# All transfers of a dilated convolution moved into one fixed order on one DMA queue

## Chip, cores, metric

One core of one Trainium2 chip. The metric is the device time of one execution in microseconds (us). Ratios in this text are computed as the mean time of one kernel's fast runs over the mean time of the fast runs of the kernel before in the same rounds on the same chip, so they are not quite the ratio of the medians that stand beside them. Some executions of a kernel run slower than the rest: one that is over 1.5% above the fastest of its kernel is called slow here (the slow state). Slow runs are left out of the ratios, but not out of the medians. The interval beside a ratio is its 95% interval.

## The reference

A 3x3 convolution with dilation 2 and padding 2, in float32: 16 images of 64 channels of 64x64, to 128 output channels.

```python
x_pad = np.pad(x, ((0, 0), (0, 0), (pad, pad), (pad, pad)), mode='constant')   # pad = 2
for b, co, ci, kh, kw in ...:                     # loops, cut
    output[b, co] += weight[co, ci, kh, kw] * x_pad[b, ci, kh*2:kh*2+h, kw*2:kw*2+w]
```

16.8 MB of images and 0.3 MB of weights come in, 33.55 MB go out.

## The kernel before

Two images make a pair (64 + 64 channels fill the 128 partitions); a pair is computed in four groups of 16 rows, 32 groups in all. Each group's sums go through three PSUM tiles, of which DVE adds two to a copy of the third (`p_sb`, made by ACT) into the output tile. Inputs arrive as float32 (`x32`, 3 buffers, 2 MB each) and are cast by ACT to float16, a quarter of a pair at a time (`cast(c)`, c counts quarters). Output tiles have 3 buffers of 4 MB.

```python
def load(pb, cuts=(0, H), queue=nc.sync):
    x32_tiles[pb] = fpool.tile([P, HW], f32, tag="x32", name="x32")
    for lo, hi in zip(cuts[:-1], cuts[1:]):
        queue.dma_start(out=x32_tiles[pb][:, lo * W : hi * W], in_=x_pair[pb, :, lo * W : hi * W])
# ... cut: at the start SyncE's queue gets the weights, pair 0 in two pieces, pair 1, pair 2

def casts(G):                                   # called in each group G
    for n in range(2 if G else 3):
        c = ahead[0]
        if c >= ngroups or c > G + (7 if c < 2 * NG else 3):
            return
        cast(c)
        ahead[0] += 1
        if c % NG == NG - 1 and c // NG + XF < npairs:      # pair fully cast: its x32 buffer is free
            k = c // NG + XF
            load(k, (0, H) if k < 6 else (0, H // 2, H), queue=nc.scalar)
# ... cut: products
    if not G:
        casts(0)
    p_sb = spool.tile([P, 2 * NH], f32, tag="psb", name="p_sb")
    nc.scalar.copy(out=p_sb, in_=psP)
    if G:
        casts(G)
# ... cut: row sums and output adds on DVE
    if pb == npairs - 1:
        ...                                     # last pair: stores in half images, one piece of it cut
                                                # into 124 + 4 partitions (FOUR, of ROWS4 = 8 rows)
    elif g == NG - 1:
        store(pb, 0)                            # SyncE's queue, 2 MB each
        store(pb, 1)
```

So there are two queues: stores (and the first loads) on SyncE's, the loads of pairs 3 to 7 on ScalarE's.

## Time and profile before

| | before |
|---|---|
| time, median of 3 | 127.12 us (127.10 to 127.21) |
| profiled execution | 128.3 us, span 126.5 us |
| data moved | 50.78 MB |
| PE busy | 105.1 us, 83% |

The page of the kernel before; the rows cut the span in 40 slices of 3.16 us, digits are tenths of busy time:

```profile
PE   6894999999999999999999999999999999300000
DMA  4999999999999999999999999999999999999960
GB/s 137 375 447 435 430 425 435 425 300 430 414 420 451 430 420 425 409 446 430 417 438 414 422 420 435 427 435 420 440 420 425 440 420 440 414 412 416 426 266 23
...
q1 hardware_dynamic: 3448, 40.14, 75.4%
q10 hardware_dynamic: 1008, 10.49, 20.4%
...
PE 75%; DMA 6%; ACT 2%; issue 1%; DVE 1%; DVEq 1%; SPq 1%; ACTq 0%
```

Two engines look full. The chain of waits is three quarters PE. But look where PE stops: at slice 34 of 40, while the DMA row stays at 9 to slice 38. The chain, in order of time, ends at the last DVE add and does not follow the stores behind it:

```profile
106.14 1.28 PE psA L174 x12
...
107.52 1.23 DVE osb L237
108.74 1.13 DVEq L287
```

The stores (SyncE's queue, duration in ns, then the first and last start in us):

```profile
L188 SPq DMA_DIRECT2D out_dram<-osb x20: 332/450/1606, 23.3 to 110.3; - x20
```

The last is issued at 110.3 us, and 12 us of transfers are still queued. So the DMA engines look like what sets the time, and PE could be late by some us without harm (before_casts5 below tests that). The windows of the kernel before show one hole in a DMA stream that otherwise runs at 428 GB/s with loads alone (4 to 20 us):

```profile
core 0: us, PE busy (x) PEld busy (x) DVE busy (x) ACT busy (x) POOL busy (x), PEclk, DMA share, GB/s
22.00:24.00 2.00, 2.00 (x24) 1.18 (x22) 1.83 (x4) 1.01 (x1) 0.00 (x0) 1.00 1.04 442
24.00:26.00 2.00, 2.00 (x22) 1.06 (x20) 2.00 (x2) 0.38 (x1) 0.00 (x0) 1.00 1.03 385
26.00:28.00 2.00, 2.00 (x23) 1.08 (x20) 1.58 (x3) 1.68 (x2) 0.00 (x0) 1.00 0.98 270
...
123.00:124.00 1.00, 0.00 (x0) 0.00 (x0) 0.00 (x0) 0.00 (x0) 0.00 (x0) 0.50 0.16 66
124.00:125.00 1.00, 0.00 (x0) 0.00 (x0) 0.00 (x0) 0.00 (x0) 0.00 (x0) 0.50 0.06 25
```

At 26:28 the DMA share is 0.98, yet only 270 GB/s move: the engines are busy with packets that take longer. This text calls it the slow stretch. At 124:125 the share is 0.06, one engine of sixteen: a straggler.

### The profile page before, as it was taken

Reading aid. Unit: us, or ns where it says so; the run is one execution under the profiler, and the core shown is the slowest. Engines: PE = TensorE matmul, PEld = TensorE weight load, DVE = VectorE, ACT = ScalarE, POOL = GpSimd, SP = SyncE. Lnnn points to the kernel's source line nnn. Section 1 sums busy time; section 2 is a strip of 40 time slices with the busy share of each in tenths; the row PEclk is TensorE's granted clock in tenths of the full one; section 3 lists DMA queues with packets and bytes.
Section 4 is the critical chain, followed back from the end, with each engine's and each line's share of the span. In section 5 each row is a group of like instructions: output and inputs, shape, how many; then the busy total and the mean of one; then the engine's idle time right before and its main releaser. Section 6 shows DMA issues by size and latency. Waiting matters only on the chain.

```text
span 126.5 us, 2335 instructions
## 1 busy us (share of the span) xinstructions
PE 105.1 (83%) x1000; PEld 56.2 (44%) x1000; DVE 90.7 (72%) x103; ACT 65.0 (51%) x68; POOL 2.3 (2%) x8
## 2 busy tenths in 40 slices
PE   6894999999999999999999999999999999300000
PEld 2251555555555555555555555555556555100000
DVE  0560998988898889898969898888888887700000
ACT  4287893366656665766486666666666533000000
POOL 2400000000000000000000000000000000000000
PEclk9999999999999999999999999999999999965555
DMA  4999999999999999999999999999999999999960
GB/s 137 375 447 435 430 425 435 425 300 430 414 420 451 430 420 425 409 446 430 417 438 414 422 420 435 427 435 420 440 420 425 440 420 440 414 412 416 426 266 23
DMA packets 4466, 50.78 MB, mean 401 GB/s; under 512 B 488, under 2 KB 488, under 8 KB 1000
## 3 DMA queue, kind: packets, MB, share of 16 engines
q1 hardware_dynamic: 3448, 40.14, 75.4%
q10 hardware_dynamic: 1008, 10.49, 20.4%
q8 instruction: 8, 0.13, 0.4%
q14 instruction: 2, 0.02, 0.0%
HBM read 17.07 MB, written 33.55 MB: 400 GB/s over the span
## 4 chain that ended last, share of the span: by engine, by line
PE 75%; DMA 6%; ACT 2%; issue 1%; DVE 1%; DVEq 1%; SPq 1%; ACTq 0%
PE psA L174 30%; PE psB L174 29%; PE psP L174 16%; DMA x<-in_x_dram 6%; DVE osb L237 1%; DVEq L287 1%; ACT p_sb L230 1%; ACT x L73 1%; SPq L64 0%; ACTq L64 0%; SPq L88 0%; DVEq L237 0%
## 5 line engine op out<-in xcount | busy, mean ns | idle before, releaser
L174 PEld LDWEIGHTS <-w_sb 64*128 64x128 f16 x960 | 54.2, 94 | 46.9 <-issue 2.1
L230 ACT COPY p_sb<-psP 128x1024 f32<-128x1024 f32 x32 | 32.4, 1012 | 37.5 <-PE psP L174 18.1
L237 DVE TENSOR_TENSOR osb<-psA,p_sb 128x1024 f32<-128x1024 f32 x32 | 39.2, 1224 | 14.2 <-PE psA L174 8.4
L174 PE MATMUL psA<-x,w_sb 64*128 64x496 f16 (+3 forms) x384 | 45.1, 365 | 0.0
L174 PE MATMUL psB<-x,w_sb 64*128 64x496 f16 (+3 forms) x384 | 45.1, 365 | 0.0
L237 DVE TENSOR_TENSOR osb<-psB,p_sb 128x1024 f32<-128x1024 f32 x32 | 39.1, 1221 | 0.0
L73 ACT CAST x<-x 128x1024 f16<-128x1024 f32 (+2 forms) x31 | 32.1, 1044 | 0.4 <-DMA x<-in_x_dram 0.4
L174 PE MATMUL psP<-xs,w_sb 64*128 64x496 f16 (+1 forms) x192 | 26.0, 371 | 1.8 <-ACT p_sb L230 1.8
L85 DVE TENSOR_TENSOR xs<-x 128x512 f16<-128x512 f16 x32 | 13.3, 416 | 0.7 <-ACT x L73 0.7
L101 PE MATMUL dm<-zero 128*128 128x512 f16 x10 | 4.6, 580 | 1.2 <-DVE zero L93 1.2
L111 DVE CAST wd<-w 128x192 f16<-128x192 f32 x1 | 0.5, 507 | 2.6 <-DMA w<-in_weight_dram 2.6
L101 PEld LDWEIGHTS <-zero 128*128 128x128 f16 x10 | 1.1, 123 | 2.6 <-issue 1.3
L124 PEld LDWEIGHTS <-wd 128*64 128x64 f16 x30 | 1.0, 118 | 2.3 <-DVE wd L111 1.2
L124 PE MATMUL wt<-ident,wd 128*64 128x128 f16 x30 | 1.6, 241 | 0.3 <-DVE wd L111 0.3
L113 ACT ACT_TABLE_LOAD x1 | 1.3, 1283 | 0.7 <-PEq L273 0.7
L136 ACT CAST w_sb<-wt 128x384 f16<-128x384 f32 x1 | 0.5, 480 | 1.8 <-PE wt L124 1.8
L113 ACT CAST wd<-w 128x192 f16<-128x192 f32 x1 | 0.5, 542 | 1.7 <-DMA w<-in_weight_dram 1.7
L138 DVE CAST w_sb<-wt 128x384 f16<-128x384 f32 x1 | 0.6, 558 | 0.9 <-PE wt L124 0.9
L93 DVE MEMSET zero<- 128x256 uint32 x1 | 0.3, 272 | 0.9 <-PEq L273 0.9
L112 POOL TENSOR_TENSOR wd<-w 128x192 f16<-128x192 f32 x1 | 0.8, 801 | 2.5 <-DMA w<-in_weight_dram 2.5
L115 POOL CAST wd<-w 128x192 f16<-128x192 f32 x1 | 0.8, 815 | 0.0
L114 DVE TENSOR_TENSOR wd<-w 128x192 f16<-128x192 f32 x1 | 0.8, 799 | 0.0
(11 smaller groups left out, 3.6 us busy)
## 6 DMA issues: line engine op xcount, KB each, us to landing
out_dram<-osb SPq DMA_DIRECT2D x14, 2048.0 KB, 17.4
x<-in_x_dram ACTq DMA_DIRECT2D x3, 2048.0 KB, 14.6
x<-in_x_dram SPq DMA_DIRECT2D x2, 2048.0 KB, 11.7
x<-in_x_dram ACTq DMA_DIRECT2D x4, 1024.0 KB, 19.9
out_dram<-osb SPq DMA_DIRECT2D x3, 1024.0 KB, 14.1
x<-in_x_dram SPq DMA_DIRECT2D x1, 1088.0 KB, 5.5
x<-in_x_dram SPq DMA_DIRECT2D x1, 960.0 KB, 7.3
out_dram<-osb SPq DMA_DIRECT2D x1, 768.0 KB, 15.6
```

Of the source, the lines that this page charges most:

```text
L73: nc.scalar.copy(out=x16_tiles[pb][:, lo * W : hi * W], in_=x32_tiles[pb][:, lo * W : hi * W])
L85: nc.vector.tensor_tensor(out=s, in0=v[:, :, 0], in1=v[:, :, 1], op=add)
L101: nc.tensor.matmul(out=dm[:, 0:512], lhsT=zero[:, 0:P], rhs=zero)
L112: nc.gpsimd.tensor_tensor(out=wdv[:, 3], in0=wv[:, 0], in1=wv[:, 1], op=sub)
L113: nc.scalar.copy(out=wdv[:, 2], in_=wv[:, 0])
L114: nc.vector.tensor_tensor(out=wdv[:, 1], in0=wv[:, 2], in1=wv[:, 1], op=sub)
L115: nc.gpsimd.tensor_copy(out=wdv[:, 4], in_=wv[:, 2])
L124: nc.tensor.matmul(out=wts[k % 3][r * CI : (r + 1) * CI, c0 + j * CO : c0 + (j + 1) * CO], lhsT=wd[:, t * CI : (t + 1) * CI], rhs=ident,)
L174: nc.tensor.matmul(out=po, lhsT=w_sb[pp, t * CO : (t + 1) * CO], rhs=rhs, start=first and j == 1, stop=last and j == 2,)
L230: nc.scalar.copy(out=p_sb, in_=psP)
L237: nc.vector.tensor_tensor(out=o[:, :, b0 : b0 + NBLK, e], in0=ps.rearrange("p (m b q) -> p m b q", m=2, q=2 * W), in1=pv, op=add,)
L287: with _tile.TileContext(nc) as tc:
```

## The change

The intent: one queue, so that each transfer runs at full rate in a chosen order, none slowed by a later one: four pairs in, the first pair out in halves with the fifth pair's load behind it, then a load and two stores in turn. Casts from pair 2 on may run two groups earlier, so that buffers come free in time.

```diff
-    def load(pb, cuts=(0, H), queue=nc.sync):
+    def load(pb, cuts=(0, H)):
...
-            queue.dma_start(
+            nc.sync.dma_start(
...
-            if c >= ngroups or c > G + (7 if c < 2 * NG else 3):
+            if c >= ngroups or c > G + (7 if c < 2 * NG else 5):
                 return
             cast(c)
             ahead[0] += 1
-            if c % NG == NG - 1 and c // NG + XF < npairs:
-                k = c // NG + XF
-                load(k, (0, H) if k < 6 else (0, H // 2, H), queue=nc.scalar)
...
-        if pb == npairs - 1:
+        if G == 0:
+            load(XF)
+        if g == NG - 1 and 0 < pb < npairs - XF - 1:
+            load(pb + XF + 1)
+        if pb in (0, npairs - 1):
             if g % 2 == 1:
                 store(pb, 0, (g - 1) * GR, (g + 1) * GR)
-                if g == 1:
+                if pb and g == 1:
...
+            if G == NG - 1:
+                load(XF + 1)
         elif g == NG - 1:
```

## The prediction

> **What bounds the kernel now.** The DMA engines. In the 40-slice page DMA reads 9 from slice 2 to slice 38, at 410 to 450 GB/s. The kernel moves 50.34 MB of data; at the rate of its steady stretches (426 GB/s in 64:93 mixed, 428 GB/s in 96:119 with stores alone, 428 GB/s early with loads alone) that is 118 us of the 126.5 us span. The rest: 1.6 us before the first packet, about 1 us at the start (302 to 348 GB/s in 2:5 while the weights come in small packets), a dip to about 306 GB/s in 25:28 (windows) in which the engines are busy but x packets take 0.7 to 1.36 us instead of 0.61 (worth about 0.9 us), and about 4 us after 122 us, where a straggling engine drains and the last receipt comes in. The Trainium skill ("DMA: Bandwidth & Descriptors", Specifications) puts the fabric ceiling at 435 GB/s; the trace agrees with 426 to 428.
>
> The chain of waits is 75% PE, but it ends there at 107 to 109 us; the last store is issued at 110.3 us and what is left is the DMA backlog, 5 MB or 12 us.
>
> **What the change does.** Same bytes, same packets in size (loads split into 8 KB a partition become whole, the first pair's stores become 8 KB: as many). The seven loads leave ACT's queue; each cost ACT 0.33 us of issue (two of them 1.1 and 1.5 us). Only one is on the PE chain: 0.38 us at 10.9 us, ahead of the first p_sb copy; compute starts about 0.4 us earlier, hidden by the DMA backlog. Casts of pair 2 start two groups earlier.
>
> The skill (same page, "Issuing engines are not separate DMA queues") says both queues run on the same 16 engines and interleave; one queue should not change the rate. In this trace mixed and single-queue stretches differ by under 1%.
>
> **Does the fixed order open a gap?** Costed from bytes moved by the time each store comes ready: at 17.3 us (first half of pair 0 done) about 2.2 MB of loads are still queued; at 23 us 2.0 MB; at 35.5 us (pair 1) over 3 MB, against 1.3 MB before; at 97.5 us (pair 6) 2.2 MB, 5 us. The loads waiting for casts 11, 15 and 19 come free at about 31, 43 and 56 us, before their turn. Output buffers come free 3 us or more before reuse. I expect no idle gap on the DMA engines, no new PE wait, and the PE end within 1 us of 108.5.
>
> **The gain** can then only be the dip at 25:28, at most 0.9 us. It sits just after the first stores were issued (23.3 us) beside a load on the other queue. If it is the price of the first writes it returns; if the meeting of two queues, it goes. Half each: minus 0.45 us. 127.12 - 0.45 gives about 126.7 us.
>
> **Signs.** Right: DMA 9 in slices 2 to 38; GB/s near 428 in every steady stretch; q10 gone; last store issue near 110 us. Wrong: a slice of DMA below 8 in the middle (starved queue), PE waits on x loads, or the output add waiting for a store.
>
> **What would make it wrong.** A transfer held behind one that isn't ready; switching between loads and stores costing rate; the straggling engine at the end moving by over 1 us.
>
> Predicted 126.7 us, 8 in 10 between 125.7 and 127.8; faster by over 2% 0.05, within 2% 0.91, slower 0.04.

(A recount of the trace gives 427 GB/s in 64:93 and 422 in 96:119, where the prediction has 426 and 428; mixed and single-queue stretches then differ by up to 1.5%, not by under 1%. By our estimate that adds 0.3 us to the 118 us of its sum: 23 us at 422 in place of 428.)

## The result, and the profile after

| | before | after |
|---|---|---|
| time, median (same rounds) | 127.16 us (127.10 to 127.43, 4 runs) | 126.75 us (126.67 to 127.05, 4 runs) |
| ratio of the fast runs | | 0.9968, 95% interval 0.9946 to 0.9989 |
| profiled execution | 128.3 us | 126.76 us |
| last store issued | 110.3 us | 109.6 us |

The same within 2%; the gain is 0.4 us. (The profiled run of before was 1.2 us slower than its median, so spans of the two traces are not to be subtracted.) The page after:

```profile
PE   6996999999999999999999999999999999400000
DMA  4999999899999999999999999999999999999991
GB/s 145 373 427 456 435 420 399 299 425 422 446 438 430 425 420 440 422 430 420 435 425 433 430 430 430 420 425 425 446 430 425 430 420 425 425 433 411 424 387 76
...
q1 hardware_dynamic: 4456, 50.63, 96.6%
...
PE 76%; DMA 6%; ACT 2%; DVE 1%; DVEq 1%; SPq 1%; issue 0%
```

q10 (ScalarE's queue) is gone; the DMA row is full as before. The chain ends 0.7 us earlier (DVE's last step in it at 106.77 in place of 107.52), and so does the last store's issue (109.6 for 110.3; in the second pair of traces, before_again and after_again, 110.1 for 111.0):

```profile
106.77 1.23 DVE osb L234
108.00 1.13 DVEq L290
```

```profile
L185 SPq DMA_DIRECT2D out_dram<-osb x22: 332/432/712, 16.6 to 109.6; - x22
```

Where compute gained is seen at its start. Before, ScalarE issued a load between its last cast and the first `p_sb` copy; after, the copy follows the cast at once (both timelines are cut at 10.5 us):

```profile
9.96 0.93 ACT L73 CAST x<-x 128x896 f16<-128x896 f32 x1
10.92 0.38 ACTq L64 DMA_DIRECT2D x<-in_x_dram  x1
11.34 1.01 ACT L230 COPY p_sb<-psP 128x1024 f32<-128x1024 f32 x1 [0.45 <-ACT x L73]
```

```profile
9.76 0.93 ACT L73 CAST x<-x 128x896 f16<-128x896 f32 x1
10.60 1.00 ACT L227 COPY p_sb<-psP 128x1024 f32<-128x1024 f32 x1
```

The windows after:

```profile
20.00:22.00 2.00, 2.00 (x24) 1.14 (x21) 1.82 (x2) 1.19 (x2) 0.00 (x0) 1.00 1.25 393
22.00:24.00 2.00, 2.00 (x24) 1.12 (x20) 1.83 (x3) 1.86 (x2) 0.00 (x0) 1.00 0.66 217
24.00:26.00 2.00, 2.00 (x22) 1.08 (x20) 1.80 (x3) 1.08 (x2) 0.00 (x0) 1.00 1.01 426
...
123.00:124.00 1.00, 0.00 (x0) 0.00 (x0) 0.00 (x0) 0.00 (x0) 0.00 (x0) 0.50 0.10 41
124.00:125.00 1.00, 0.00 (x0) 0.00 (x0) 0.00 (x0) 0.00 (x0) 0.00 (x0) 0.50 0.00 0
```

The slow stretch is there again, at 21 to 24 us, now with a single queue. (A packet counts in the window where it starts, so a share over 1 ahead of one under 1 is long packets, not idleness.) The straggler ends sooner in this trace; by how much differs from run to run, as the table below shows. One new wait showed, in the timeline of DVE:

```profile
85.24 1.23 DVE L234 TENSOR_TENSOR osb<-psA,p_sb 128x1024 f32<-128x1024 f32 x1 [0.52 <-DMA out_dram<-osb]
```

An output buffer came free 0.5 us late. It will have cost nothing here, as the stores queued at the end are much longer than that.

Three numbers are used below, all worked out from the packet records of each trace. *Slow time*: for the 20 to 30 us stretch, the sum over packets of what each took over its usual time (611 ns for 16 KB, 309 ns for 8 KB, the medians), divided by the 16 engines. *Last engine*: the end of the last packet. *Mean engine*: the ends of the last 16 semaphore packets (4 bytes each, one for each engine), averaged. Where a second number stands, it is a further stretch outside 20 to 30 us. The profiled runs:

```
kernel                   run us   slow time us   mean engine   last engine   run - last
before                   128.30   1.00           122.67        125.37        2.93
before_again             127.86   1.04           122.85        124.79        3.07
before_casts5            127.54   1.08           122.59        124.47        3.07
after                    126.76   1.02           122.36        123.82        2.94
after_again              127.06   1.10           122.62        123.99        3.07
old_order_one_queue      127.03   1.01           122.51        124.00        3.03
old_order_one_queue_2    127.65   1.01           122.70        124.71        2.94
after_early_store        127.87   0.94           122.58        124.74        3.13
after_early_store_sp     128.78   0.98           122.75        125.73        3.05   (slow state)
after_half_four          127.08   1.00           122.50        124.01        3.07
after_casts3             127.62   0.79 + 0.90    123.21        124.58        3.04   (second stretch at 42 us)
after_store_first        127.89   1.90           123.54        124.96        2.93   (two stretches)
new_order_two_queues     130.48   1.04 + 1.24    125.48        127.56        2.92   (slow state; more at 38 to 47 us)
after_early_bulk         130.80   1.87 + 0.48    126.46        127.74        3.06   (two, and one at 9 to 14 us; 2.4 us more of data)
```

In every trace the run's time is the last engine's end plus 2.9 to 3.1 us. So the time is the DMA engines' work, with whatever the slowest of the sixteen adds. Leaving out the two slow runs and the last kernel with its extra data, that last part (last engine less mean engine) goes from 1.4 to 2.7 us.

### The profile page after: what moved, and what is told of

It reads as the page before. It is cut to its first block, busy times and chain, and to the rows that moved or that the text cites. A ratio compares the mean times of both kernels' runs of the same rounds, so it can differ in the third digit from the quotient of the medians.

```text
span 125.0 us, 2339 instructions
## 1 busy us (share of the span) xinstructions
PE 105.1 (84%) x1000; PEld 56.0 (45%) x1000; DVE 90.8 (73%) x103; ACT 64.9 (52%) x68; POOL 2.2 (2%) x8
## 4 chain that ended last, share of the span: by engine, by line
PE 76%; DMA 6%; ACT 2%; DVE 1%; DVEq 1%; SPq 1%; issue 0%
PE psA L171 31%; PE psB L171 30%; PE psP L171 16%; DMA x<-in_x_dram 6%; ACT x L73 2%; DVE osb L234 1%; DVEq L290 1%; ACT p_sb L227 1%; SPq L64 0%; SPq L88 0%; DVEq L234 0%
## 6 DMA issues: line engine op xcount, KB each, us to landing
out_dram<-osb SPq DMA_DIRECT2D x12, 2048.0 KB, 19.3
```

## The experiments

Twelve further runs were made, of nine edited kernels (one of them twice) and of the two kernels unedited; all gave correct results. One more kernel, the two-queue version of the changed one with the old cast limit, was not run, and nothing of it is on record. The author gives as the reason a deadlock, which the program's order bears out: the load of pair 5 stands in ScalarE's program at the end of group 7, where the old limit has let casts up to number 10 through, and it would wait for cast 11 behind it. So with two queues this order needs the earlier casts.

### Controls: after_again and before_again

No edit. For the changed kernel:

> Control, the changed kernel once more, for a tighter ratio and a second trace. Expected: ratio to the kernel before 0.996 to 0.998, the slow stretch of loads (rate under 300 GB/s for about 2 us) again at 21 to 24 us just ahead of the first store packets, worth 1.0 us per DMA engine. If the 0.3% gain was chance, the ratio is 1.000 within 0.001.

Median 126.99 us against 127.22, ratio 0.9969, interval 0.9924 to 1.0014; slow time 1.10 us at 21 to 24 us. For the kernel before:

> Control: the kernel before, twice. Ratio 1.000 within 0.002; what it differs by is the noise of such a comparison. Its second trace: slow stretch at 25 to 28 us, 1.0 us; the last DMA engine ends about 3.0 us before the run's time, near 124.2 us (the first trace, of a run 1.2 us above the median, had 125.4).

Median 127.82 against 127.36, ratio 1.0014, interval 0.9978 to 1.0050. The runs spread more here than in the first comparison (126.95 to 128.02 for the kernel before, against 127.10 to 127.43). The last engine ended at 124.8, not 124.2, in a run 0.5 us above the median. The gain of 0.3% came out in two comparisons with the same point value, but its second interval holds 1: it is at the edge of what such runs resolve.

### Queue or order: old_order_one_queue and its repeat

```diff
-                load(k, (0, H) if k < 6 else (0, H // 2, H), queue=nc.scalar)
+                load(k, (0, H) if k < 6 else (0, H // 2, H), queue=nc.sync)
```

> The kernel before with its loads issued from SyncE at the same places of the program: one queue, old order and old cast schedule. Theory Q (the gain is the single queue: loads and stores no longer share each DMA engine packet by packet): ratio 0.997. Theory O (the gain is the order of the transfers, or the earlier casts): ratio 1.000. Both: slow stretch stays, 1.0 us.

127.35 us, ratio 0.9990, interval 0.9936 to 1.0045; runs from 126.59 to 128.62, too noisy. The slow time was 1.01 us, at 26 to 29 us. The ten traces at hand by then suggested a theory: the last engine ended 1.4 to 1.5 us behind the mean wherever only one queue was used, 1.9 to 2.7 where two were. The repeat was to test it:

> Repeat of the old order on one queue, whose first timing was too noisy. Theory Q (the gain is the single queue, through a more even finish of the 16 DMA engines): ratio 0.995 to 0.998, the last engine ends 1.3 to 1.6 us after the mean of the engines (with two queues it was 1.9 to 2.7). Theory O (the gain is the order): ratio 1.000, 1.9 us or more.

127.12 us against 127.33, ratio 0.9988, interval 0.9955 to 1.0021. The last engine ended 2.0 us behind the mean. The ratio lies between the two theories and its interval holds both, and the number that theory Q named came out on the wrong side. So did a later trace, after_early_bulk below, with two queues and 1.3 us. Over all twelve fast traces, six of the seven with one queue have 1.4 to 1.5 us and one has 2.0; four of the five with two have 1.9 to 2.7 and one has 1.3. The present run and three of those four were 0.3 to 1.2 us above their kernel's median, so the lag may belong to a slower run and not to the queues. That theory is not kept.

### New order, two queues: new_order_two_queues

```diff
-            load(XF)
+            load(XF, queue=nc.scalar)
...           # the same for load(pb + XF + 1) and load(XF + 1)
```

> The changed kernel with its fourth to eighth loads on ScalarE's queue at the same places of the program. Theory Q: ratio 1.000 (gain gone). Theory O: 0.997 (gain kept). Both: slow stretch stays, 1.0 us.

128.42 us (slow runs up to 130.6 included), ratio 1.0047, interval 0.9986 to 1.0107: it holds theory Q's 1.000 and not theory O's 0.997. But something else happened in this kernel too, so it tests neither. ScalarE's timeline and a window of the profiled run show it. (That run was slow. The wait is not told from this run alone: the next experiment shows it in a fast one.)

```profile
19.19 1.01 ACT L227 COPY p_sb<-psP 128x1024 f32<-128x1024 f32 x1 [0.42 <-ACT x L73]
26.14 1.15 ACT L73 CAST x<-x 128x1152 f16<-128x1152 f32 x1 [5.94 <-DMA x<-in_x_dram]
```

```profile
24.00:26.00 2.00, 0.50 (x6) 0.11 (x2) 0.00 (x0) 0.00 (x0) 0.00 (x0) 1.00 0.95 401
26.00:28.00 2.00, 0.00 (x0) 0.00 (x0) 0.00 (x0) 1.86 (x2) 0.00 (x0) 0.82 0.99 418
```

The first cast of pair 2 is wanted at 20 us, and ScalarE waits 5.9 us for its input; with it the `p_sb` copies wait, and PE stands idle through 26:28. The fourth load, on its own queue, takes its turns on the DMA engines beside the third: by the packet records the third pair's last packet ended at 25.2 us here, at 18.4 us in the changed kernel. PE ended at 114.9 us, against 107.8 in the changed kernel, and in this slow run the DMA engines lost time as well: by the packet records they stood idle for about 0.7 us at 38 to 40 us, and slow stretches at 38 to 47 us took another 1.2 us. How much of this the fast runs had is not known, as none of them was traced.

### The early casts alone: before_casts5

```diff
-            if c >= ngroups or c > G + (7 if c < 2 * NG else 3):
+            if c >= ngroups or c > G + (7 if c < 2 * NG else 5):
```

> The kernel before with only the cast limit of the change (casts of pair 2 onward two groups earlier), loads still on ScalarE's queue. Theory S (with two queues the third pair's load shares the DMA engines with the fourth and lands near 22 to 26 us, so a cast wanted at 20 us blocks ScalarE and with it the p_sb copies): ScalarE waits 2 to 5 us for x near 20 us and PE with it; the time still changes by less than 1% as the DMA backlog at the end absorbs it, ratio 1.000 to 1.005. Rival (the stall in the two-queue run came of the store order): no wait over 1 us, ratio 1.000.

As theory S said, in a fast run:

```profile
19.74 1.01 ACT L230 COPY p_sb<-psP 128x1024 f32<-128x1024 f32 x1 [0.46 <-PE psP L174]
24.59 1.15 ACT L73 CAST x<-x 128x1152 f16<-128x1152 f32 x1 [3.83 <-DMA x<-in_x_dram]
```

```profile
L188 SPq DMA_DIRECT2D out_dram<-osb x20: 332/459/1127, 23.4 to 112.2; - x20
```

ScalarE waited 3.8 us, and the last store was issued 1.9 us later than before (112.2 for 110.3). The time: 127.20 us, ratio 0.9995, interval 0.9965 to 1.0025. Nearly 2 us of compute (1.5% of the time), lost on what the chain of waits calls 75% of the kernel, cost nothing that these runs can see. This is the clearest proof that the DMA engines, not PE, set the time.

### Without the early casts: after_casts3

```diff
-            if c >= ngroups or c > G + (7 if c < 2 * NG else 5):
+            if c >= ngroups or c > G + (7 if c < 2 * NG else 3):
```

> The changed kernel with the old cast limit. Theory F (the fixed order needs the early casts, as the sixth load waits for cast 11 in the queue ahead of pair 1's stores): SyncE issues the sixth load near 36.5 us instead of 30, with the fifth load all but done (37.5 us): a slot at 37 to 39 us with DMA under 0.9, 0.5 to 1.5 us lost, ratio 0.999 to 1.008. Rival (the slack was enough anyway): no such slot, ratio 0.997.

127.92 us, ratio 1.0035, interval 1.0006 to 1.0064: slower, by the amount that theory F gave, but not in its way. The sixth load was issued at 36.4 us and the engines did not idle at 37 to 39. Instead a second slow stretch came up, in that load, ahead of pair 1's stores:

```profile
40.00:42.00 2.00, 2.00 (x22) 1.09 (x20) 1.59 (x3) 1.29 (x2) 0.00 (x0) 1.00 1.03 426
42.00:44.00 2.00, 2.00 (x22) 1.07 (x20) 2.00 (x2) 0.79 (x2) 0.00 (x0) 1.00 1.08 295
44.00:46.00 2.00, 2.00 (x23) 1.14 (x20) 1.58 (x3) 1.84 (x2) 0.00 (x0) 1.00 0.93 393
```

0.90 us of slow time; as the first stretch was shorter here (0.79), that is 0.6 to 0.7 us more than in the changed kernel's traces, and the mean engine ended 0.6 to 0.85 us later than in those two. So slow time is worth about its length in time, and it is not tied to the first stores alone.

### What makes the slow stretch: four tries

A small store, early, on ScalarE's queue and then on SyncE's:

```diff
+    z32 = wpool.tile([P, W], f32, name="z32")
+    nc.gpsimd.memset(z32, 0.0)
+    nc.scalar.dma_start(out=out_img[B - 1, :, HW - W : HW], in_=z32)     # second run: nc.sync
```

> The changed kernel plus one 32 KB store of zeros (256 B a partition, to a row that the last store overwrites) at the start, on ScalarE's idle queue. Theory W (the slow stretch is a one-time price of the first write to HBM): the stretch leaves 21 to 24 us, loads run at 428 GB/s there; some slowness near 2 to 4 us instead; ratio 0.990 to 0.997, best if it hides in the start. Theory B (it is what happens when a bulk store first comes up behind or beside bulk loads): the stretch stays at 21 to 24 us with 1.0 us lost, ratio as the changed kernel or 0.1% worse.

> The changed kernel with the 32 KB early store on SyncE's own queue, behind the third load. Theory Q (any use of a second queue makes the finish uneven, which is why the early store on ScalarE's queue cost 0.4 us): ratio 0.996 to 0.998, last engine 1.3 to 1.6 us after the mean. Rival (the extra store itself costs, wherever it is queued): ratio 1.001, last engine about 2 us after the mean. Slow stretch stays at 21 to 24 us.

127.46 us, ratio 1.0010 (0.9966 to 1.0054), and 127.29 us, ratio 0.9982 (0.9945 to 1.0018). The stretch stayed in both; in the first:

```profile
21.00:23.00 2.00, 2.00 (x24) 1.17 (x22) 2.00 (x2) 1.05 (x2) 0.00 (x0) 1.00 0.95 254
```

So it is not a price paid by the first write of all. (The first one's store moved at 2.9 to 3.4 us, the second one's at 17.8 to 19.3 us, so the first is the sharper test.) The second kernel's profiled run was slow, with the last engine 3.0 us behind the mean although it uses one queue only; whether the small store costs anything is within the noise.

The first stores ahead of the fourth load:

```diff
-        if G == 0:
+        if G == 2:                       # now behind the stores of group 1
             load(XF)
```

> The changed kernel with the fourth load behind the first pair's first two half-image stores instead of ahead of them, so the first stores reach the DMA engines near 18 us instead of 23.4. Theory V (the slow stretch belongs to the first bulk stores coming up behind loads, wherever they stand): it moves to 15.5 to 18.5 us, 1.0 us lost, ratio 0.997. Theory T (it belongs to the time, near 22 to 26 us after the start): it stays there. If it vanishes (third rival: it needs a load started late in the run ahead of the stores) the ratio is 0.989.

127.64 us, ratio 1.0007 (0.9971 to 1.0044). The stretch neither moved to 15.5 to 18.5 us nor stayed as it was: there were two.

```profile
19.00:21.00 2.00, 2.00 (x22) 1.09 (x20) 1.58 (x3) 1.57 (x2) 0.00 (x0) 1.00 1.02 430
21.00:23.00 2.00, 2.00 (x25) 1.17 (x23) 2.00 (x3) 1.30 (x2) 0.00 (x0) 1.00 1.04 369
...
27.00:29.00 2.00, 2.00 (x22) 1.07 (x20) 2.00 (x3) 0.79 (x2) 0.00 (x0) 1.00 1.02 254
```

By the packet records the first 1 MB store, at 17.9 to 20.9 us, ran at full rate (310 ns for 8 KB), the second averaged 370 ns, and the fourth load behind them 783 ns for 16 KB. Full rate in the first megabyte speaks again against a price of first writing.

A bulk store, early:

```diff
+    nc.scalar.dma_start(out=out_img[B - 1, :, HW // 2 : HW], in_=x32_tiles[0][:, 0 : HW // 2])
     nc.scalar.copy(out=x16_tiles[0][:, 0 : 8 * W], in_=x32_tiles[0][:, 0 : 8 * W])
```

> Wrong data on purpose in a region that is overwritten later: the changed kernel plus a 1 MB store from ScalarE's queue as soon as the first half image has landed, near 6 us. It adds 2.4 us of DMA work (1.05 MB at 428 GB/s), ratio about 1.016. Theory V (the slow stretch is the first bulk store meeting loads, once): it shows within 5 us of that store, and not ahead of the first pair's stores near 23 to 27 us. Rival: it stays ahead of the first pair's stores, 1.0 us, so neither the first write nor the first bulk write makes it.

131.17 us, ratio 1.0300 (1.0256 to 1.0345), not 1.016: the added megabyte's 2.4 us came with about 1.3 us of further slow time. A small slow stretch (0.48 us at 9 to 14 us) came about the start of the early store (issued at 7.0 us, its packets between the loads' at 10.7 to 19.2 us), and the one ahead of the first pair's stores stayed and had grown:

```profile
21.00:23.00 2.00, 2.00 (x24) 1.16 (x22) 1.99 (x3) 1.54 (x3) 0.00 (x0) 1.00 0.90 295
23.00:25.00 2.00, 2.00 (x24) 1.19 (x22) 2.00 (x4) 2.00 (x3) 0.00 (x0) 1.00 1.07 385
25.00:27.00 2.00, 2.00 (x22) 1.07 (x20) 2.00 (x2) 1.19 (x2) 0.00 (x0) 1.00 0.97 229
```

What is shown: the stretch is in all fourteen traces, with one queue or two, near where loads and the first pair's stores meet (20 to 29 us), 0.8 to 1.9 us of slow time each. It does not need two queues, it is not a price of the first write, and it is not paid once: four traces show more than one. Most later changes from load to store (pairs 2 and 3, at 45 to 75 us in every trace of the new order on one queue) show none: at most 0.12 us in any 5 us there. What makes it stays open.

### A try at a better version: after_half_four

```diff
-    ROWS4 = 8
+    ROWS4 = 4
```

> A try at a better version: the changed kernel with the piece of the last pair that goes to four DMA engines only halved (4 rows in place of 8). In the one-queue traces the engines that took that piece are among the last to end. If they set the end: last engine about 0.4 us earlier, ratio 0.993 to 0.995. If not: ratio 0.996 to 1.000.

127.13 us, ratio 0.9990 (0.9953 to 1.0027); the last engine ended at 124.01 us, as in the changed kernel. No gain: that piece does not set the end, or what it gives is lost in the noise. (The packet records kept here don't name the engine, so which engines end last is inferred at best.) No version here beat the changed kernel.

## Why the prediction was right, and where it was not

**The bound: right, and shown.** DMA reads full from slice 2 to the tail in both pages, and the rate outside the slow stretch is unchanged. Slowing PE by nearly 2 us (before_casts5) cost nothing; 0.6 to 0.7 us more of slow DMA time (after_casts3) went with an end 0.6 to 0.85 us later. With the same bytes and one set of engines there was little to win, so 126.7 us was forecast and 126.75 us measured.

**One queue doesn't change the rate: right.** The prediction took this from the Trainium skill, "DMA: Bandwidth & Descriptors", section "Issuing engines are not separate DMA queues": all issuers share the same 16 DMA engines. The trace agrees: at 36 to 60 us, with loads and stores mixed, 429 GB/s before on two queues, 428 after on one, and 427 for the old order on one.

**No gap from the fixed order: right but for the output buffers.** From slice 2 on, every slice reads DMA 8 or 9 until the tail. "Output buffers come free 3 us or more before reuse" was too generous: one came 0.5 us late (the DVE wait at 85.24 us, a wait that the prediction lists among its signs of being wrong), and 1.7 us late in after_casts3. PE did not wait for either: from the first `p_sb` copy to its end it took 97.2 and 97.3 us, as before (97.2).

**Compute 0.4 us earlier: right.** The first `p_sb` copy starts 0.45 us after the cast ahead of it has ended in all three traces with loads on ScalarE's queue at that place (before, before_again, before_casts5), and 0.09 us before that end in the changed kernel's two and in the old order's two on one queue: 0.54 us, for 0.4 forecast. (The last store's issue moved by 0.7 us, from 110.3 to 109.6, because in that trace of the kernel before the casts also ended 0.2 us later; they differ by up to 0.9 us among these traces.) The backlog hid it, as predicted.

**"The gain can then only be the dip": this step failed.** The prediction weighed two causes half and half, minus 0.45 us. Measured: the slow stretch kept its size (1.00 us before, 1.02 and 1.10 after), so this term was 0. The stretch did return, as in the prediction's other half, but not for the reason given there, "the price of the first writes": the early stores and the full-rate first megabyte speak against that cause. The total came out right because about 0.4 us was gained elsewhere, if it was gained at all. That part of the hit is luck.

**Where the 0.4 us came from: not settled.** The run's time follows the last DMA engine, and that one's lag behind the mean varies by up to 0.75 us between two runs of one kernel (2.69 and 1.94 us in the kernel before). The single queue alone gave 0.999 twice, the whole change 0.997 twice (and 0.999 with the small edit of after_half_four); the intervals overlap. The sum in the prediction had no term for the straggler, only a line of doubt about it.

**What the change's parts are for.** The early casts need the single queue: without it the third pair's load shares the engines with the fourth and comes too late for them (waits of 3.8 and 5.9 us on ScalarE). The fixed order does better with the early casts: without them a second slow stretch appears. What moves compute 0.5 us earlier is neither of them, but that the loads leave ScalarE: the old order on one queue shows it too. In a kernel whose time compute does not set, that gives nothing that these runs can see.

## What to carry to other kernels

When the DMA row is full from start to end, the order of transfers moves waits about and has little to win: here only the slow stretch (about 1 us) and the straggler (1.4 to 2.7 us behind the mean). Test a claim of "PE bound" by looking at what is still queued when PE stops, or by delaying PE on purpose. On shared DMA engines a later load on a second queue takes turns from an earlier one, so "issue early" can make the transfer that is wanted first land later (25.2 us for 18.4 here). Before explaining a few tenths of a per cent, run the kernel before against itself: here that alone gave 1.0014, with an interval of 0.36% on either side.

## What the Trainium skill lacked or had wrong

- "DMA: Bandwidth & Descriptors", Specifications, lists an HBM limit of about 358 GB/s for one core and doesn't say there when it holds. It was not the limit of this program on one core: loads alone, both mixed and stores alone held 428, 427 and 422 GB/s (the kernel before at 4 to 20, 64 to 93 and 96 to 119 us). The same page's section "Measured", for a core whose neighbour is idle, has 425 GB/s, which fits, as does its fabric ceiling of 435.
- The same page, "Issuing engines are not separate DMA queues", says that several issuers save only issue time. It doesn't say what they can cost: the third pair's load ended at 25.2 us with the fourth on a second queue, at 18.4 us with both on one. (Its section "Queues, rings and completion order", on turns between queues, fits that.)
- No page tells of the slow stretch: near the first bulk stores, 16 KB packets that average 0.7 to 1.2 us in place of 0.61 for 2 to 4 us, with the engines busy, 0.8 to 1.9 us of slow time in each of 14 traces.
- No page gives how far the slowest of the 16 DMA engines ends behind their mean. Here it was 1.4 to 2.7 us in eleven traces of fast runs, and the time was that last end plus 2.9 to 3.1 us in all fourteen.
